# Queries and keys asked for two or three units ahead in a two-layer attention kernel

## The chip, the cores and the metric

The kernel runs on one core of a Trainium2 chip. The metric is device time in microseconds (us) of one execution of the whole program.

## What is computed

Two layers over 1024 latent tokens and 256 context tokens, model width 1024, all in fp32. Each layer is: adaptive norm, an input projection that also yields a gate, attention, gate, output projection, residual. Layer 0 is grouped-query attention (16 heads of 64 over 4 key heads, rotary positions, norms on queries and keys); there the context tokens attend too, to context only. Layer 1 is latent attention (16 heads, 64 + 32 wide). Cut to the attention, with the names of the reference:

```python
def gqa_attend(q, k, v):
    s = jnp.einsum('bqhgd,bkhd->bhgqk', q, k).astype(jnp.float32) * (GQA_HEAD_DIM ** -0.5)
    p = jax.nn.softmax(s, axis=-1).astype(v.dtype)
    return jnp.einsum('bhgqk,bkhd->bqhgd', p, v)

k_all = jnp.concatenate([kc, k], axis=1)
v_all = jnp.concatenate([vc, v], axis=1)
o = sweep_query_blocks(lambda qb: gqa_attend(qb, k_all, v_all), q).reshape(B, S, GQA_WIDTH)
y = (o * jax.nn.silu(g)) @ p["w_out"]
oc = gqa_attend(qc, kc, vc).reshape(B, L, GQA_WIDTH)
```

## The kernel before

Stages follow each other: modulation and norm, projections of layer 0 (queries, keys, values and gate go to DRAM), attention of layer 0, its output projection with the norm of layer 1, projections of layer 1, attention of layer 1, output projection. The change touches the two attention stages, which share the class `Attention`.

The work of attention is cut into **units**. Layer 0 has 20: 16 of one head with all 1024 latent queries against 10 key tiles of 128, and 4 short ones of context queries (one key head's four heads, 2 key tiles). The short ones stand at places 4, 9, 18 and 19, counted from 0; the first five units (0 to 4) share the first key head. Layer 1 has 16 units, each of one head and 10 key tiles.

Each unit needs two passes. First the **maxima**: for each of 8 blocks of 128 queries a product with the latent keys (`mx`, L364) whose rows VectorE reduces to a maximum (`mA`, L366), and two products with the context keys (L370, reduced to `mB`, L372); a context unit has only the last two. All use one PSUM tile. The maxima are transposed (L385), negated into a row (`crow`, L387) and written by DMA into an extra row of the unit's queries (L388), so that the second pass subtracts them inside the matmul. Second the **scores** (`st`, L423) key tile by key tile, the exponential on ScalarE (`p`, L426), sums over the keys on POOL (`acp`, L449) and VectorE (`acd`, L453), and the product with the values (`av`, L471). At a unit's end ScalarE copies `av` to `os` (L493, two buffers), TensorE spreads the sums over partitions (L515), ScalarE copies those to `rb` (L517), and by way of small DMAs (`cs` L519, `rrow` L524, `rb` L528), a reciprocal and two POOL products (L531, L532) the result is stored (`od`, L536).

TensorE's order is that of the program text; the other engines' orders are set by a scheduler. The loop `run` goes over pairs of key tiles; one key tile is a step. For each pair it asks `maxima` for all maxima up to `step - base + 1 + lead` (lead is 14), runs what has come due, issues the `av` of two pairs back, asks for one maximum more, and issues the scores of the pair. So the maxima run about a unit and a half ahead of the scores. `maxima` starts a unit, which means asking for its queries and keys, only when it has no maxima left in its list; and it starts none beyond the limit `t + 1 + ahead`, t being the place of the unit whose scores are issued and `ahead` 2. Since it starts a unit at the moment in which it needs it, its first `mx` follows the load directly in the program.

Queries are two tiles, QA (high halves twice, filled by two DMAs, L837) and QB (low halves and the row of maxima, L838) in layer 0; L846 and L847 are the same for context units. There are three sets of them (`qbufs=3`). Keys KA and KB are shared by the units of a key head (two sets). In layer 1 QH, QL, KH and KL belong to a unit (three sets, L1085 to L1091). All these DMAs are issued by SyncE's queue, in one order.

The transpose of the maxima writes into `spare`, the `av` tile of the unit that finished last, or into the `mx` tile when there is none yet. The spread sums of that same unit (L515) go into columns 0 to 255 of the same tile.

Of the kernel before, what the change touches and what calls it, by code (L numbers as in the profile page):

```python
# [14 lines left out]
ALU = mybir.AluOpType  # L15
# [4 lines left out]
P = 128  # L20
# [10 lines left out]
def raw(ap):  # L31
    return ap.bitcast(F32)
# [3 lines left out]
def hybrid_kernel(ctx: ExitStack, tc: tile.TileContext, ins: dict, out: bass.AP):  # L36
    nc = tc.nc
    pe, act, dve, pool, sp = nc.tensor, nc.scalar, nc.vector, nc.gpsimd, nc.sync
# [10 lines left out]
    ident = const.tile([P, P], F32, name="ident")  # L49
# [24 lines left out]
    def in_order(engine):  # L74

        return tc.manual_schedule(engines={engine})
# [240 lines left out]
    class Attention:  # L317
# [20 lines left out]
        def open_late(self, st, stp):  # L338
            l = self.l
            self.op = st.enter_context(tc.tile_pool(name=f"op{l}", bufs=2, reuse_waits="tile"))  # L340
            self.vp = stp.enter_context(tc.tile_pool(name=f"vp{l}", bufs=1 + l, reuse_waits="tile"))
            self.pp = stp.enter_context(tc.tile_pool(name=f"pp{l}", bufs=8, reuse_waits="tile"))
            self.ap = stp.enter_context(tc.tile_pool(name=f"ap{l}", bufs=2, reuse_waits="tile"))
            self.rd = st.enter_context(tc.tile_pool(name=f"rd{l}", bufs=4, space=DRAM))
            self.ps_s = stp.enter_context(tc.tile_pool(name=f"pss{l}", bufs=2, space=PSUM, reuse_waits="tile"))
            self.ps_o = stp.enter_context(tc.tile_pool(name=f"pso{l}", bufs=2, space=PSUM, reuse_waits="tile"))
# [27 lines left out]
        def do_shift(self, u):  # L374
            s = self.state[id(u)]
            c = s["mB"]
            if u["kind"] == "lat":
                c = self.sm.tile([P, 8], F32, name="mC", tag="mC")
                dve.tensor_max(c, s["mA"], s["mB"])

            def turn():
                t = self.spare
                if t is None:
                    t = self.ps_m.tile([P, 1024], F32, name="mx", tag="mx")
                pe.transpose(t[:8, :P], c, ident)  # L385
                r = self.sm.tile([8, P], F32R, name="crow", tag="crow")
                dve.tensor_scalar(r, t[:8, :P], -1.0, None, op0=ALU.mult)  # L387
                sp.dma_start(raw(s["crow"]), raw(r))  # L388

            self.later((2, turn))  # L390
# [13 lines left out]
        def maxima(self, upto, limit):  # L404

            while self.done < upto:
                if not self.todo:
                    if self.started >= min(limit, len(self.units)):
                        break
                    self.start_unit()  # L410
                u, m = self.todo.pop(0)
                self.done += 1
                self.do_max(u, m)
                if m == ("ctx", 1):
                    self.do_shift(u)
# [127 lines left out]
        def run(self, lead, ahead, extra):  # L543

            held = []
            base = self.step
            pairs = [(t, u, u["kts"][i:i + 2]) for t, u in enumerate(self.units) for i in range(0, len(u["kts"]), 2)]
            with in_order(mybir.EngineType.PE):
                for t, u, kts in pairs:
                    if kts[0] == u["kts"][0]:  # L550
                        for v in self.units[t:t + 2]:
                            self.load_v(v)
                    self.maxima(self.step - base + 1 + lead, t + 1 + ahead)
                    self.run_deferred(self.step)
                    if len(held) == 2:
                        self.do_av(*held.pop(0))
                    self.maxima(self.step - base + 2 + lead, t + 1 + ahead)
                    held.append((u, [(kt, self.do_scores(u, kt)) for kt in kts]))
                    if extra and self.step - base >= 5:
                        extra.pop(0)()  # L560
                    self.step += 2
                for h in held:
                    self.do_av(*h)
            self.run_deferred(self.step + self.lag)
# [250 lines left out]


    def l0_load(u, at):
        qp, kp = at.qp, at.kp
        g = u["g"]
        r = slice(64 * (g % 2), 64 * (g % 2) + 64)  # L820
        lat = u["kind"] == "lat"
        if g not in at.kcache:
            KA = kp.tile([P, NT], F32R, name="KA", tag="KA")
            KB = kp.tile([65, NT], F32R, name="KB", tag="KB")
            sp.dma_start(raw(KA[0:64, :]), k0h[g // 2, r, :])
            sp.dma_start(raw(KA[64:128, :]), k0l[g // 2, r, :])
            sp.dma_start(raw(KB[0:64, :]), k0h[g // 2, r, :])
            pool.memset(raw(KB[64:65, :]), 1.0)
            at.kcache[g] = dict(KA=KA, KB=KB)
        KA, KB = at.kcache[g]["KA"], at.kcache[g]["KB"]  # L830
        QA = qp.tile([P, NL], F32R, name="QA", tag="QA")
        QB = qp.tile([65, NL], F32R, name="QB", tag="QB")
        if lat:
            h = u["h"]
            r = slice(64 * (h % 2), 64 * (h % 2) + 64)
            for j in range(2):
                sp.dma_start(raw(QA[64 * j:64 * j + 64, :]), q0h[h // 2, r, :NL])  # L837
            sp.dma_start(raw(QB[0:64, :]), q0l[h // 2, r, :NL])  # L838
        else:
            for par in range(2):  # L840
                r = slice(64 * par, 64 * par + 64)
                cs = slice(512 * par, 512 * par + 512)
                sh = q0h[2 * g:2 * g + 2, r, NL:].rearrange("a p n -> p a n")
                sl = q0l[2 * g:2 * g + 2, r, NL:].rearrange("a p n -> p a n")
                for j in range(2):
                    sp.dma_start(raw(QA[64 * j:64 * j + 64, cs]).rearrange("p (a n) -> p a n", a=2), sh)  # L846
                sp.dma_start(raw(QB[0:64, cs]).rearrange("p (a n) -> p a n", a=2), sl)  # L847
        return dict(KA=KA, KB=KB, QA=QA, QB=QB, mq=QA, mk=KA, crow=QB[64:65, :])

    def l0_scores(s, kt):  # L850
        ks = slice(kt * P, (kt + 1) * P)
        return [(s["KA"][:, ks], lambda n: s["QA"][:, n * 512:(n + 1) * 512]),
                (s["KB"][:, ks], lambda n: s["QB"][:, n * 512:(n + 1) * 512])]
# [13 lines left out]
    def gate_path(l, c, w, hT, nt, ps_mm, wk):  # L867
        for m in range(4):
            for s0 in range(0, nt, 512):
                gate_slice(l, c, m, s0, min(512, nt - s0), w, hT, ps_mm, wk)  # L870

    at = Attention(0, units, dict(scale=0.125, load=l0_load, scores=l0_scores, kbufs=2, qbufs=3, vw=256))
    stE = ExitStack()
    with tc.tile_pool(name="wkg0a", bufs=4, **right) as wkg:
# [12 lines left out]
    pieces = []  # L887
    wo = [load_weight(ins["l0_w_out"], KT, 512 * n, 512, 0, todo=pieces) for n in range(2)]
    stL, stLP = ExitStack(), ExitStack()
    at.open_late(stL, stLP)  # L890
    at.run(14, 2, pieces)
    stLP.close()
    stE.close()

# [206 lines left out]
    for p_ in range(8):  # L1101
        for par in range(2):
# [3 lines left out]
    at = Attention(1, units, dict(scale=float(96 ** -0.5), load=l1_load, scores=l1_scores,  # L1106
                                  kbufs=3, qbufs=3, vw=128))
# [133 lines left out]
    pieces = []  # L1241
# [58 lines left out]
```

## Time and profile before

| what | value |
|---|---|
| median of 3 runs | 1938.57 us (1936.34 to 1942.59) |
| the profiled execution | 1934.7 us, span 1932.8 us |
| mean granted clock of TensorE | 0.971 |
| TensorE busy | 1806.6 us (93%) |
| attention of layer 0, 402 to 898 us | 495.41 us, TensorE busy 441.79 |
| attention of layer 1, 1357 to 1838 us | 481.00 us, TensorE busy 471.27 |

The page gives busy time by engine over one profiled execution. A window gives the same for a stretch. In a timeline each row is a group of instructions with its start, its duration and, in brackets, the idle time of the engine before it and what ended that. PE is TensorE, DVE VectorE, ACT ScalarE, POOL GpSimd, SP SyncE and SPq its queue of DMA issues. A releaser printed as "issue" means that the profile shows nothing that the engine waited for.

### The profile page before, as it was taken

To read this page: it belongs to the slowest core of one execution; us is meant where nothing else is said; L and a number is where in the kernel's file an instruction comes from. 1 tells how busy PE (TensorE), PEld (TensorE's weight loads), DVE (VectorE), ACT (ScalarE), POOL (GpSimd) and SP (SyncE) were. 2 spreads that over 40 slices of the span, in tenths; PEclk is the share of its full clock that TensorE was granted. 3 is DMA by queue.
4 is the path that set the end of the run, shared out by engine and by line. 5 is a ranking of instruction groups with operands and counts; after the bars stand their busy time and mean duration, and the time that the engine had idled before them with its cause. 6 is when DMAs were issued, how large, how long until landed. Compare 5 with 4: busy or idle time off the path is not lost. (4 is left out here: it accounts for less than half of the span.)

```text
span 1932.8 us, 23525 instructions
## 1 busy us (share of the span) xinstructions
PE 1806.6 (93%) x8360; PEld 1225.4 (63%) x8360; DVE 1003.9 (52%) x1494; ACT 633.1 (33%) x942; POOL 959.9 (50%) x648
## 2 busy tenths in 40 slices
PE   7889999988798899987998999999999999999999
PEld 3676668754344445543787889887555555555577
DVE  3754551355464566643456567765555454555332
ACT  2421221133233334432224453331433333333410
POOL 1553431156556467764224455342666657666521
PEclk9999999999898899998999999999999999999999
DMA  7556753332132222223443494766434334342152
GB/s 273 172 172 197 240 161 109 113 104 55 44 87 66 70 57 59 66 66 103 138 140 86 134 267 135 207 188 177 123 81 107 93 82 120 81 107 71 28 186 98
DMA packets 220765, 235.00 MB, mean 122 GB/s; under 512 B 34024, under 2 KB 162776, under 8 KB 220648
## 3 DMA queue, kind: packets, MB, share of 16 engines
q1 hardware_dynamic: 220648, 233.50, 42.7%
q8 instruction: 66, 1.08, 0.2%
q14 instruction: 51, 0.42, 0.1%
HBM read 159.51 MB, written 73.63 MB: 121 GB/s over the span
## 5 line engine op out<-in xcount | busy, mean ns | idle before, releaser
L366 DVE TENSOR_REDUCE mA<-mx 128x1 f32<-128x1024 f32 x256 | 313.3, 1224 | 378.2 <-PE mx L364 377.9
L426 ACT ACTIVATE p<-st 128x1024 f32<-128x1024 f32 x328 | 328.1, 1024 | 552.4 <-PE st L423 552.3
L449 POOL TENSOR_TENSOR acp<-acp,p 128x1024 f32<-128x1024 f32 x156 | 370.2, 2373 | 238.0 <-ACT p L426 232.5
L471 PE MATMUL av<-p,v 128*64 128x512 f32 x1312 | 330.7, 625 | 1.0 <-ACT rb L517 1.0
L129 POOL TENSOR_TENSOR wb<-wraw,wa 128x512 fp32r<-128x512 f32 (+3 forms) x69 | 90.6, 1332 | 175.8 <-ACT wa L148 175.2
L471 PEld LDWEIGHTS av<-p,v 128*64 128x64 f32 x1312 | 82.1, 140 | 149.6 <-issue 139.8
L364 PE MATMUL mx<-KA,QA 128*128 128x512 f32 x256 | 95.8, 458 | 40.2 <-DVE mA L366 14.5
L86 PE MATMUL mm<-wa,hh 128*128 128x512 f32 (+2 forms) x320 | 123.2, 385 | 2.5 <-ACT hh L286 2.5
L372 DVE TENSOR_REDUCE mB<-mx 128x4 f32<-128x1024 f32 x72 | 87.8, 1219 | 68.1 <-PE mx L370 67.8
L87 PE MATMUL mm<-wb,hh 128*128 128x512 f32 (+2 forms) x320 | 118.5, 371 | 0.0
L88 PE MATMUL mm<-wa,hl 128*128 128x512 f32 (+2 forms) x320 | 118.0, 370 | 0.0
L86 PE MATMUL y<-wa,oh 128*128 128x512 f32 x288 | 114.2, 396 | 3.5 <-ACT oh L594 3.5
L449 POOL TENSOR_TENSOR acp<-p 128x1024 f32<-128x1024 f32 x32 | 76.5, 2391 | 74.5 <-ACT p L426 73.8
L87 PE MATMUL y<-wb,oh 128*128 128x512 f32 x288 | 113.1, 393 | 0.0
L88 PE MATMUL y<-wa,ol 128*128 128x512 f32 x288 | 112.4, 391 | 0.0
L364 PEld LDWEIGHTS mx<-KA,QA 128*128 128x128 f32 x256 | 45.1, 203 | 103.2 <-DVE mA L366 52.4
L423 PE MATMUL st<-QA,KA 128*128 128x512 f32 x336 | 107.8, 402 | 0.0
L423 PE MATMUL st<-QB,KB 65*128 65x512 f32 x336 | 106.5, 398 | 0.0
L423 PE MATMUL st<-QH,KH 97*128 97x512 f32 x320 | 102.2, 400 | 1.3 <-DMA QH<-crow 1.3
L423 PE MATMUL st<-QL,KH 96*128 96x512 f32 x320 | 102.2, 400 | 0.6 <-DVE gth L311 0.6
L86 PE MATMUL mm<-hh,wa 128*128 128x512 f32 x256 | 102.2, 399 | 0.2 <-DVE qt L1182 0.2
L88 PE MATMUL mm<-hh,wb 128*128 128x512 f32 x256 | 101.8, 398 | 0.0
(212 smaller groups left out, 3383.9 us busy)
## 6 DMA issues: line engine op xcount, KB each, us to landing
mraw<-in_l_w_mod SPq DMA_DIRECT2D x96, 256.0 KB
wraw<-in_l_w_in SPq DMA_DIRECT2D x28, 512.0 KB
rb<-rrow SPq DMA_DIRECT2D x72, 128.0 KB
xt<-in_x SPq DMA_DIRECT2D x16, 512.0 KB
wraw<-in_l_w_out SPq DMA_DIRECT2D x16, 512.0 KB
sgd<-gth SPq DMA_DIRECT2D x32, 256.0 KB
QA<-q0h SPq DMA_DIRECT2D x32, 256.0 KB
sg<-sgd SPq DMA_DIRECT2D x64, 128.0 KB
```

The lines of the kernel that those rows point to most:

```text
L86: pe.matmul(ps, lhsT=lh(k), rhs=rh(k), start=first and i == 0, stop=False)
L87: pe.matmul(ps, lhsT=lh(k), rhs=rl(k), start=False, stop=False)
L88: pe.matmul(ps, lhsT=ll(k), rhs=rh(k), start=False, stop=last and i == len(ks) - 1)
L129: eng.tensor_sub(lo, a, b)
L364: pe.matmul(m[:, n * 512:(n + 1) * 512], lhsT=s["mq"][:, i * P:(i + 1) * P], rhs=s["mk"][:, n * 512:(n + 1) * 512], start=True, stop=True)
L366: dve.reduce_max(s["mA"][:, i:i + 1], m, axis=AX.X)
L372: dve.reduce_max(s["mB"][:, 4 * i:4 * i + 4], m.rearrange("p (a b) -> p a b", a=4), axis=AX.X)
L423: pe.matmul(ps[:, n * 512:(n + 1) * 512], lhsT=lh, rhs=rf(n), start=(j == 0), stop=(j == len(prods) - 1))
L426: act.activation(p, ps, AF.Exp, scale=self.ops["scale"])
L449: pool.tensor_add(t, a, p)
L471: pe.matmul(s["av"][64 * n:64 * n + 64, :], lhsT=s["v"][:, kt, u["vc"]:u["vc"] + 64], rhs=p[:, n * 512:(n + 1) * 512], start=kt == kts[0], ...
```

## The change

Four edits. In `run`, the first pair of each unit now starts all units up to the limit, before any maximum is asked for. In layer 0 `ahead` is 3 instead of 2, and a fourth set of queries is taken from a pool of its own: units 3, 7, 11 and so on use it. The transpose of the maxima goes to columns 256 to 383 of its tile. The loop in `maxima` is written differently and does the same.

```diff
         def open_late(self, st, stp):
             l = self.l
             self.op = st.enter_context(tc.tile_pool(name=f"op{l}", bufs=2, reuse_waits="tile"))
+            if not l:
+
+                self.qp2 = stp.enter_context(tc.tile_pool(name="qp0b", bufs=1, reuse_waits="tile"))
...
                 if t is None:
                     t = self.ps_m.tile([P, 1024], F32, name="mx", tag="mx")
-                pe.transpose(t[:8, :P], c, ident)
+                t = t[:8, 256:384]
+                pe.transpose(t, c, ident)
                 r = self.sm.tile([8, P], F32R, name="crow", tag="crow")
-                dve.tensor_scalar(r, t[:8, :P], -1.0, None, op0=ALU.mult)
+                dve.tensor_scalar(r, t, -1.0, None, op0=ALU.mult)
...
             while self.done < upto:
+                if not self.todo and self.started < min(limit, len(self.units)):
+                    self.start_unit()
                 if not self.todo:
-                    if self.started >= min(limit, len(self.units)):
-                        break
-                    self.start_unit()
+                    break
...
                         for v in self.units[t:t + 2]:
                             self.load_v(v)
+                        while self.started < min(t + 1 + ahead, len(self.units)):
+                            self.start_unit()
                     self.maxima(self.step - base + 1 + lead, t + 1 + ahead)
...
     def l0_load(u, at):
-        qp, kp = at.qp, at.kp
+        kp = at.kp
...
+        qp = at.qp if at.started % 4 < 3 else at.qp2
         QA = qp.tile([P, NL], F32R, name="QA", tag="QA")
...
     at.open_late(stL, stLP)
-    at.run(14, 2, pieces)
+    at.run(14, 3, pieces)
```

The last edit is layer 0's call; layer 1's stays at 2. The lines below L341 move down by 3 to 7 in the changed kernel (L364 is L367 there, L423 is L427, L837 is L844).

What the change does to TensorE's order, at the end of unit 2 in layer 0. Before, with `mB` the maxima of the context unit 4, and the six `mx` those of unit 5:

```order
L385 MATMUL av<-ident,mB 8x128
L471 MATMUL av<-p,v 64x512 x4
L423 MATMUL st<-QA,KA 128x512 x2
L423 MATMUL st<-QB,KB 128x512 x2
L423 MATMUL st<-QA,KA 128x512 x2
L423 MATMUL st<-QB,KB 128x512 x2
L364 MATMUL mx<-KA,QA 128x512 x6
L471 MATMUL av<-p,v 64x512 x4
L364 MATMUL mx<-KA,QA 128x512 x2
```

The same place after the change:

```order
L367 MATMUL mx<-KA,QA 128x512 x2
L389 MATMUL av<-ident,mB 8x128
L475 MATMUL av<-p,v 64x512 x4
L367 MATMUL mx<-KA,QA 128x512 x2
L427 MATMUL st<-QA,KA 128x512 x2
L427 MATMUL st<-QB,KB 128x512 x2
L427 MATMUL st<-QA,KA 128x512 x2
L427 MATMUL st<-QB,KB 128x512 x2
L367 MATMUL mx<-KA,QA 128x512 x2
L475 MATMUL av<-p,v 64x512 x4
```

The six matmuls of three maxima that stood together now stand two by two, the first four of them ahead of unit 2's last scores. It is the same at the ends of units 3, 7 and 8, and with the two context maxima of unit 19 at the end of unit 16.

SyncE's queue around the load of unit 5, with the numbers of the tiles. Before (cs and rrow and rb are those of unit 1; the two rows of maxima go to units 3 and 4; QA_3982 and QB_3983 are unit 5's):

```order
L519 DMA cs_3832<-rb_3827 32x1x8 x4
L388 DMA QB_3690<-crow_3919 1x8x128
L524 DMA rrow_3831<-cr_3948 128x8
L388 DMA QB_3895<-crow_3952 1x8x128
L528 DMA rb_3827<-rrow_3831 64x512 x2
L837 DMA QA_3982<-q0h_81 64x1024 x2
L838 DMA QB_3983<-q0l_82 64x1024
L536 DMA od0_96<-os_3825 64x512 x2
```

After (the first rows are those of unit 0; unit 5's queries are QA_3799 and QB_3800; the last cs is unit 1's):

```order
L523 DMA cs_3636<-rb_3631 32x1x8 x4
L392 DMA QB_3408<-crow_3722 1x8x128
L528 DMA rrow_3635<-cr_3759 128x8
L532 DMA rb_3631<-rrow_3635 64x512 x2
L844 DMA QA_3799<-q0h_81 64x1024 x2
L845 DMA QB_3800<-q0l_82 64x1024
L540 DMA od0_96<-os_3629 64x512 x2
L512 DMA sg_4048<-sgd0_94 64x512 x2
L523 DMA cs_3857<-rb_3852 32x1x8 x4
```

Unit 5's load has moved forward by one unit's DMAs: it stands behind unit 0's sums instead of unit 1's.

The transpose of unit 3's maxima and the spread sums ahead of it in TensorE's order, with the semaphores that each waits for. Before (av_3653 is unit 1's tile, av_3864 unit 2's; the mx is unit 4's):

```order
L515 MATMUL av_3653<-acp_3629,twos_76 32x256 [waits Pool_49]
L515 MATMUL av_3653<-acp_3629,twos_76 32x256 x3
L385 MATMUL av_3653<-ident_69,mC_3875 8x128 [waits DVE_49,Activation_49]
L471 MATMUL av_3864<-p_3842,v_3402 64x512 x2
L471 MATMUL av_3864<-p_3851,v_3402 64x512 x2
L370 MATMUL mx_3926<-KA_2934,QA_3894 128x256 [waits DMAHW4_49,DMAHW3_49,DVE_49]
```

After:

```order
L519 MATMUL av_3672<-acp_3648,twos_76 32x256 [waits Pool_49]
L519 MATMUL av_3672<-acp_3648,twos_76 32x256 x3
L389 MATMUL av_3672<-ident_69,mC_3900 8x128 [waits DVE_49,Activation_49]
L475 MATMUL av_3889<-p_3867,v_3405 64x512 x2
L475 MATMUL av_3889<-p_3876,v_3405 64x512 x2
L373 MATMUL mx_3942<-KA_2934,QA_3580 128x256 [waits DMAHW4_49,DMAHW3_49,DVE_49]
```

The order of these is unchanged, and the transpose names the same two semaphores, VectorE's and ScalarE's.

## Prediction

> **What bounds the kernel now.** I read the busy rows of the page first, then TensorE's waits, then the two attention stages as windows, and then the places of the waits in the timeline. The page gives busy time by engine, and the granted TensorE clock in 40 slices.
>
> ```profile
> PE 1806.6 (93%) x8360; PEld 1225.4 (63%) x8360; DVE 1003.9 (52%) x1494; ACT 633.1 (33%) x942; POOL 959.9 (50%) x648
> PEclk9999999999898899998999999999999999999999
> ```
>
> TensorE (PE) is the bound: 1806.6 of 1932.8 us. Eights stand among the nines in slices 11, 13, 14 and 19 (48.3 us each), so between 483 and 918 us PE runs slower at times. The two attention stages as windows (busy us of PE, PEld, DVE, ACT, POOL; then clock and DMA):
>
> ```profile
> 402.14:897.55 495.41, 441.79 (x1881) 233.39 (x1879) 273.79 (x276) 182.64 (x207) 317.30 (x154) 0.93 0.25 63
> 1357.00:1838.00 481.00, 471.27 (x2081) 278.06 (x2081) 244.92 (x262) 181.24 (x197) 314.42 (x158) 0.99 0.36 89
> 750.00:800.00 50.00, 48.70 (x218) 26.20 (x219) 31.79 (x34) 20.10 (x23) 36.06 (x19) 1.00 0.25 62
> ```
>
> Layer 1's attention leaves PE idle for 9.7 of 481 us. Layer 0's leaves it idle for 53.6 of 495.4 us, at clock 0.93; yet a stretch inside it (750 to 800) has 1.3 us of idle in 50 at clock 1.00. So layer 0 loses time in a few places. TensorE's waits name the candidates (total us, times, longest):
>
> ```profile
> PE mx L364 <- DVE mA L366: 14.9, 12, 1.3
> PE av L385 <- ACT rb L517: 13.4, 26, 0.9
> PE mx L364 <- DMA QA<-q0h: 8.9, 2, 4.5
> PE mx L364 <- issue: 8.8, 2, 4.5
> PE mx L370 <- DMA QA<-q0h: 4.5, 2, 3.1
> ```
>
> One such place in PE's timeline (start, duration; in brackets the idle before it), and the queue's Q load just ahead:
>
> ```profile
> 475.62 0.73 PE L423 MATMUL st<-QA,KA 128*128 128x512 f32 x2
> ...
> 482.24 1.19 PE L364 MATMUL mx<-KA,QA 128*128 128x512 f32 x2 [4.48 <-issue]
> 484.75 1.22 PE L364 MATMUL mx<-KA,QA 128*128 128x512 f32 x2 [1.32 <-DVE mA L366]
> 487.29 1.22 PE L364 MATMUL mx<-KA,QA 128*128 128x512 f32 x2 [1.32 <-DVE mA L366]
> 488.44 3.36 PE L471 MATMUL av<-p,v 128*64 128x512 f32 x8
> 491.73 0.73 PE L364 MATMUL mx<-KA,QA 128*128 128x512 f32 x2
> 492.30 0.62 PE L423 MATMUL st<-QA,KA 128*128 128x512 f32 x2
> ...
> 494.16 0.63 PE L364 MATMUL mx<-KA,QA 128*128 128x512 f32 x2
> 494.72 1.94 PE L471 MATMUL av<-p,v 128*64 128x512 f32 x8
> 496.59 0.72 PE L364 MATMUL mx<-KA,QA 128*128 128x512 f32 x2
> ```
>
> ```profile
> 452.12 1.29 SPq L846 DMA_DIRECT2D QA<-q0h  x2
> 477.32 1.08 SPq L837 DMA_DIRECT2D QA<-q0h  x2
> ```
>
> PE finishes a unit's last scores, then sits 4.48 us until the queries of unit 5, asked for at 477.32, have landed. Three maxima then follow with nothing between them, so that two wait 1.32 us each for VectorE's reduction, and the next eight av matmuls take 3.36 us where the same eight take 1.94 us later: after the stall PE is slow. The code says why three at once: the limit t+3 keeps unit 5 from starting during unit 2, the count falls behind, and the first call of unit 3 catches up. That is so only near the short context units (4 and 9), whose two maxima bring the next unit forward.
>
> **The change part by part.** First the price of one such place. The normal pair is 2 maxima, 1 av group, 1 score group. From the rows: a score group 494.16 - 492.30 = 1.86, a maximum 494.72 - 494.16 = 0.56, an av group 496.59 - 494.72 = 1.87. From 475.62 to 494.72 PE issued 2 score groups, 5 maxima and 1 av group: 3.72 + 2.80 + 1.87 = 8.4 us of work at full speed. This stretch and the three others cut at the same instructions, and a fifth at the end of the stage:
>
> ```profile
> 475.62:494.72 19.10, 11.99 (x37) 5.90 (x35) 4.89 (x4) 3.19 (x4) 12.59 (x7) 0.73 0.34 83
> 511.76:531.35 19.59, 12.49 (x36) 6.04 (x34) 4.89 (x4) 3.18 (x4) 12.94 (x8) 0.74 0.33 80
> 610.80:630.24 19.44, 12.48 (x36) 6.10 (x34) 4.90 (x4) 3.18 (x4) 12.58 (x7) 0.74 0.32 81
> 647.29:665.86 18.57, 11.49 (x36) 5.88 (x34) 4.89 (x4) 3.18 (x4) 12.93 (x8) 0.72 0.34 85
> 850.76:865.07 14.31, 9.79 (x34) 5.38 (x33) 2.45 (x2) 2.62 (x3) 12.58 (x7) 0.76 0.29 80
> ```
>
> Four stretches: 19.10 + 19.59 + 19.44 + 18.57 = 76.70, less 4 x 8.4 = 33.6, leaves **43.1 us** (7.1 us of plain idle each, the rest slow matmuls). The fifth holds 2 score groups, 1 av group and the two maxima of a context unit:
>
> ```profile
> 856.00 0.71 PE L370 MATMUL mx<-KA,QA 128*128 128x256 f32 x4 [3.10 <-DMA QA<-q0h]
> 858.12 1.19 PE L370 MATMUL mx<-KA,QA 128*128 128x256 f32 x4 [1.42 <-DMA QA<-q0h]
> ```
>
> At 0.58 us per such maximum (estimate: 4 x 256 columns, as many as the 2 x 512 that took 0.56) it is 3.72 + 1.87 + 1.16 = 6.8 us of work, and 14.31 - 6.8 = **7.5 us** lost.
>
> *The limit of layer 0 raised by one, the loop that starts units at a unit's beginning, and the fourth query set* go together. PE's order after the change has one maximum either side of each av group at all five places, so bursts are gone. In the queue, unit 5's Q load takes the slot that unit 4's had: issued at 452.12 before, some 21 us ahead of its first maximum, which would come at about 473.6. A 4.9 us load (477.32 to 482.24) is hidden by that. The fourth set is what makes it possible: the load now waits for the scores of unit 1, not of unit 2. I take the whole 43.1 + 7.5 = 50.6 us. Nothing else is late at once in place of the load: in 750 to 800 the same pattern runs with POOL busy 36.06 of 50, DVE 31.79, and PE idle 1.3. At the fifth place POOL could hold the gain back, since it lags behind at the end of layer 0:
>
> ```profile
> 849.17 9.65 POOL L449 TENSOR_TENSOR acp<-acp,p 128x1024 f32<-128x1024 f32 x4 [4.17 <-ACT p L426]
> 869.54 2.36 POOL L449 TENSOR_TENSOR acp<-p 128x1024 f32<-128x1024 f32 x1 [5.97 <-ACT p L426]
> ```
>
> But it then sat idle 5.97 us waiting for p. Moved up by 7.5 us that sum would start at 862.0, and POOL is free at 869.54 - 5.97 = 863.6: 1.6 us late for one sum, made up before the next. So the fifth counts in full.
>
> *The same loop in layer 1* has three sets of keys and queries and the old limit. There the loads wait for their buffers anyway:
>
> ```profile
> 1416.26 0.31 SPq L1091 DMA_DIRECT2D QL<-q1l  x1
> 1418.70 1.13 SPq L536 DMA_DIRECT2D od<-os  x2
> 1419.88 0.59 SPq L1085 DMA_DIRECT2D KH<-k1h  x1
> ```
>
> ```profile
> PE av L385 <- ACT rb L517: 7.5, 14, 0.9
> ```
>
> The order moves KH, QH and KL ahead of one od store: some 3 us earlier, a full unit before they are used, and the store some 3 us later at most. The second fence is the only wait of PE listed between 1400 and 1800 us; none names a load. I take 0.
>
> *The transposed maxima in columns 256 to 383.* Before, the transpose (L385) waits for ScalarE's copy of the sums (13.4 us in 26 waits), for both use columns 0 to 127 of one tile. After, the columns are apart, but the order with its waits still shows the ScalarE semaphore on every one of them. I take 0; if the wait went, it would be 13.4 us less. [...]
>
> *The rewritten loop in maxima* tests the same things in another order and issues nothing.
>
> *What the moved loads pass.* Each is 3 DMAs (6 for a context unit), no more than before. At units 2, 3, 7 and 8 they now stand between the two halves of rb or ahead of an od store, while SyncE waits for PE's scores (total, times, longest):
>
> ```profile
> SPq L837 <- PE st L423: 33.0, 11, 6.9
> 524.85 1.13 SPq L536 DMA_DIRECT2D od<-os  x2
> 538.24 0.59 ACT L493 COPY os<-av 128x512 f32<-128x512 f32 x1 [1.32 <-PE av L471]
> ```
>
> The copy at 538.24 (unit 4's) needs the store issued at 524.85 (unit 2's), 13.4 us earlier. With the stall of 511.76 to 531.35 gone the copy comes 11.2 us sooner and the store does not: 2.2 us are left for the landing, and ScalarE's exps queue behind that copy. In the new order the copy stands one exp later (over 1 us). I take 0; the bounds are 0 and the longest such wait, 6.9 us, at units 4 and 9: 13.8 us.
>
> **Sum.** The profiled execution took 1934.7 us (span 1932.8): 1934.7 - 50.6 = 1884.1. The median of the runs shown, 1938.57, is 3.9 above it; the measured median should be about **1888.0 us**. A change of 0.3% (6 us) is what a measurement of this kernel tells from none.
>
> **Rivals.** (a) *Part is given back.* The late store above costs up to 13.8 us. Also, two waits of 2.4 us stand where VectorE is late behind POOL's sums after a context unit, and each slows the next group:
>
> ```profile
> 574.76 0.73 PE L364 MATMUL mx<-KA,QA 128*128 128x512 f32 x2 [2.39 <-DVE mB L372]
> 576.77 3.57 PE L471 MATMUL av<-p,v 128*64 128x512 f32 x8
> ```
>
> That is 2.39 + (3.57 - 1.94) = 4.0 us each. Four more of them would cost 16 us; either or both give 1896 to 1918, say 1904. For it: POOL catches up in the present stalls (12.6 us busy in each). Against: 750 to 800 keeps step without any. Chance 0.16. (b) *The transposes stop waiting*: 1888.0 - 13.4 = 1874.6. Against it stand the waits in the order. 0.05. (c) *The change does not do what it says*: the early load still waits for a buffer until the burst, and all stays: 1938.6. Against it, the load stands one unit's work earlier in the order. 0.03. (d) *Slower*: every Q load of layer 0 that waits for a buffer, 16 of them (units 4 to 19), holds SyncE's queue; the rb and od DMAs behind it come late, POOL's sums queue behind the rb product, and p buffers run out. At 6.9 us each that is 16 x 6.9 = 110 us, 1888 + 110 = 1998; it decides from 50.6 / 16 = 3.2 us per load. The mean wait now is 33.0 / 11 = 3.0 us, but PE lost none of it in 750 to 800. 0.04.
>
> **The numbers.** The forecast, 1880 to 1896, has 0.72. The range 1874 to 1908 holds it, (b), and some half of (a): about 0.85. Faster by over 0.3%: 0.72 + 0.16 + 0.05 = 0.93; within 0.3%: 0.03; slower: 0.04.
>
> **What would show it.** Right: in layer 0's running stage no maximum with a bracket naming DMA QA or a 4.4 us issue; no run of three maxima; the stage's window some 50 us shorter at clock 0.98 or more; the 2.4 us waits on mB still two. The wait of the transposes on ScalarE stays at about 0.5 us, 26 times; if it is gone, (b). If a wait on an av group, on st behind os, or on mB appears new after units 4 and 9, (a). What would make me wrong is a wait in layer 0 that today's stalls cover and that I did not find; layer 1 and all stages outside attention should stay within 2 us.

## The result, and the profile after

The changed kernel takes 1890.99 us (median of 4 runs, 1887.21 to 1898.05), the kernel before 1938.59 (4 runs, 1936.34 to 1942.59). The ratio is 0.9756, with a 95% interval of 0.9723 to 0.979. The forecast was 1888.0 in a range of 1874 to 1908.

In the changed kernel's file the lines stand three or four further down: L364 is L367, L366 L369, L372 L375, L385 L389, L423 L427, L449 L453, L453 L457, L471 L475, L517 L521. The page's rows that answer to those of before:

```profile
PE 1788.6 (95%) x8360; PEld 1218.9 (65%) x8360; DVE 1008.3 (53%) x1494; ACT 632.8 (34%) x942; POOL 964.5 (51%) x648
PEclk8999999999999999998999999998999999999999
```

The eights of slices 11, 13 and 14 are gone; those that stand now, in slices 1, 19 (849 to 897 us) and 28, lie outside layer 0's attention but for the last 3 us of it. The stages as windows (span, then busy us of PE, PEld, DVE, ACT, POOL, the clock, DMA), cut where the stages of the changed kernel begin:

```profile
402.00:852.00 450.00, 425.20 (x1880) 229.32 (x1878) 279.59 (x276) 182.00 (x207) 320.07 (x153) 0.98 0.28 71
852.00:1311.50 459.50, 433.01 (x2229) 370.24 (x2229) 271.48 (x559) 157.78 (x331) 179.14 (x206) 0.97 0.57 164
1311.50:1792.00 480.50, 470.81 (x2081) 278.23 (x2081) 242.90 (x263) 181.96 (x198) 315.39 (x157) 0.99 0.35 89
```

Layer 0's attention takes 450.0 us, 45.4 less than the 495.41 of before, at a granted clock of 0.98 in place of 0.93; layer 1's 480.5 (before 481.0); the stage between the two was 1357.00 - 897.55 = 459.45 and is 459.5. The whole span went from 1932.8 to 1887.5, 45.3. So the gain lies in one stage. Where TensorE ran three maxima in a row after a 4.48 us wait, it now runs one maximum on either side of each av group:

```profile
475.61 0.62 PE L427 MATMUL st<-QA,KA 128*128 128x512 f32 x2
...
477.48 0.63 PE L367 MATMUL mx<-KA,QA 128*128 128x512 f32 x2
477.94 0.27 PE L389 MATMUL av<-ident,mB 128*8 128x128 f32 x1
478.14 1.94 PE L475 MATMUL av<-p,v 128*64 128x512 f32 x8
480.01 0.73 PE L367 MATMUL mx<-KA,QA 128*128 128x512 f32 x2
480.58 0.62 PE L427 MATMUL st<-QA,KA 128*128 128x512 f32 x2
```

and the queries of unit 5 were asked for at 456.05, 21.4 us ahead of that first maximum at 477.48:

```profile
456.05 1.08 SPq L844 DMA_DIRECT2D QA<-q0h  x2
```

TensorE's waits after: no row names QA or "issue" for a maximum any more; the transposes' wait stays.

```profile
PE av L389 <- ACT rb L521: 13.2, 26, 0.9
PE mx L367 <- DVE mB L375: 5.8, 3, 2.3
PE mx L367 <- DVE mA L369: 4.8, 6, 1.3
PE mx L389 <- DVE mA L369: 2.7, 1, 2.7
```

The last row is new: before, no transpose waited longer than 1.3 us for mA. It belongs to the first 35 us of layer 0's attention, the one stretch of the table below that is over 0.6 us longer in the changed kernel. The same transpose before, and TensorE there after:

```profile
417.05 0.27 PE L385 MATMUL mx<-ident,mC 128*8 128x128 f32 x1 [1.32 <-DVE mA L366]
417.25 1.94 PE L471 MATMUL av<-p,v 128*64 128x512 f32 x8
```

```profile
415.87 0.73 PE L367 MATMUL mx<-KA,QA 128*128 128x512 f32 x2 [1.11 <-DVE mB L375]
419.32 0.37 PE L389 MATMUL mx<-ident,mC 128*8 128x128 f32 x1 [2.73 <-DVE mA L369]
419.63 3.48 PE L475 MATMUL av<-p,v 128*64 128x512 f32 x8
```

**One row for each unit.** ScalarE copies the spread sums of every unit once (`rb`, 36 copies in each profile), so the starts of these copies give a clock by units. From them, and from TensorE's third score group of the stage (412.95 before, 412.72 after), come four spans for each kernel, in us: from that score group to the first copy (start), from the first copy to the 18th (layer 0), from there to the 21st (between), and to the 36th (layer 1). (Two expectations call that score group the fourth; it is the same row.)

| kernel | start | layer 0 | between | layer 1 |
|---|---|---|---|---|
| before | 29.67 | 454.77 | 507.96 | 435.44 |
| changed | 33.83 | 405.44 | 508.52 | 435.29 |
| before_again | 29.70 | 454.71 | 507.96 | 435.44 |
| loop_only | 34.31 | 455.37 | 510.96 | 435.28 |
| columns_only | 29.56 | 453.45 | 511.03 | 435.47 |
| no_loop | 34.73 | 409.92 | 507.16 | 435.30 |
| bursts_kept | 33.46 | 422.12 | 507.25 | 435.28 |
| no_columns | 33.81 | 406.90 | 511.50 | 434.72 |
| first_late | 33.46 | 403.91 | 509.34 | 435.26 |
| mc_one_input | 32.07 | 410.25 | 506.65 | 435.26 |
| turn_later | 30.98 | 405.62 | 516.21 | 425.82 |
| both | 31.70 | 404.04 | 515.88 | 425.83 |
| turn_l1 | 33.58 | 405.35 | 510.57 | 425.82 |
| held_load | 34.22 | 406.65 | 514.85 | 425.82 |

The change gains 454.77 - 405.44 = 49.3 us in layer 0 and loses 4.2 at its start: 2.5 of these as longer idle time of TensorE (3.84 us in that stretch, 1.32 before), the rest as slow matmuls such as the 3.48 us above. The experiments ask which edit carries the 49.3, how it splits, and what makes the 4.2.

### The profile page after: what moved, and what is told of

Its sections match the earlier page's. It is cut to its first block, busy times and chain, and to the rows that moved or that the text cites. A ratio compares the mean times of both kernels' runs of the same rounds, so it can differ in the third digit from the quotient of the medians.

```text
span 1887.5 us, 23536 instructions
## 1 busy us (share of the span) xinstructions
PE 1788.6 (95%) x8360; PEld 1218.9 (65%) x8360; DVE 1008.3 (53%) x1494; ACT 632.8 (34%) x942; POOL 964.5 (51%) x648
## 5 line engine op out<-in xcount | busy, mean ns | idle before, releaser
L369 DVE TENSOR_REDUCE mA<-mx 128x1 f32<-128x1024 f32 x256 | 313.4, 1224 | 340.5 <-PE mx L367 340.5
L453 POOL TENSOR_TENSOR acp<-acp,p 128x1024 f32<-128x1024 f32 x156 | 371.4, 2381 | 235.6 <-ACT p L430 230.0
L475 PE MATMUL av<-p,v 128*64 128x512 f32 x1312 | 324.9, 615 | 1.7 <-ACT rb L521 1.7
L475 PEld LDWEIGHTS av<-p,v 128*64 128x64 f32 x1312 | 80.9, 138 | 146.8 <-issue 136.6
L375 DVE TENSOR_REDUCE mB<-mx 128x4 f32<-128x1024 f32 x72 | 87.8, 1220 | 63.1 <-PE mx L373 63.1
L427 PE MATMUL st<-QA,KA 128*128 128x512 f32 x336 | 106.8, 399 | 0.0
L427 PE MATMUL st<-QB,KB 65*128 65x512 f32 x336 | 106.3, 398 | 0.0
L427 PE MATMUL st<-QH,KH 97*128 97x512 f32 x320 | 102.2, 400 | 1.0 <-DMA QH<-crow 1.0
L427 PE MATMUL st<-QL,KH 96*128 96x512 f32 x320 | 102.4, 401 | 0.6 <-DVE gth L311 0.6
L87 PE MATMUL mm<-hl,wa 128*128 128x512 f32 x256 | 101.9, 398 | 0.0
L367 PE MATMUL mx<-KA,QA 128*128 128x512 f32 x256 | 89.0, 429 | 13.3 <-DVE mB L375 5.8
L427 PE MATMUL st<-QH,KL 96*128 96x512 f32 x320 | 99.7, 393 | 0.0
```

The source lines that it names most:

```text
L87: pe.matmul(ps, lhsT=lh(k), rhs=rl(k), start=False, stop=False)
L367: pe.matmul(m[:, n * 512:(n + 1) * 512], lhsT=s["mq"][:, i * P:(i + 1) * P], rhs=s["mk"][:, n * 512:(n + 1) * 512], start=True, stop=True)
L369: dve.reduce_max(s["mA"][:, i:i + 1], m, axis=AX.X)
L375: dve.reduce_max(s["mB"][:, 4 * i:4 * i + 4], m.rearrange("p (a b) -> p a b", a=4), axis=AX.X)
L427: pe.matmul(ps[:, n * 512:(n + 1) * 512], lhsT=lh, rhs=rf(n), start=(j == 0), stop=(j == len(prods) - 1))
L453: pool.tensor_add(t, a, p)
```

## The experiments

Each was timed against the kernel before on the same chip; ratios are to that kernel.

**The loop alone** on the kernel before.

```diff
                             self.load_v(v)
+                        while self.started < min(t + 1 + ahead, len(self.units)):
+                            self.start_unit()
```

> The kernel before with the early start loop alone (two units ahead, three query sets, limit t+3 unchanged in effect). Theory (the early load needs the fourth query set to be early, and the limit still holds the maxima back): the 4.5 us waits for QA after units 2, 3, 7 and 8 and the pairs of 1.32 us stay, layer 0's attention stays near 495 us, 1935 to 1942 us. Rival (asking early is what counts, the set matters little): the QA waits go, 1888 to 1905 us.

Measured: 1938.17 us (10 runs, 1935.06 to 1941.54), ratio 0.9986 (0.9973 to 0.9999). The waits of before are all there:

```profile
PE mx L364 <- DVE mA L366: 14.9, 12, 1.3
PE mx L364 <- issue: 8.8, 2, 4.4
PE mx L364 <- DMA QA<-q0h: 8.7, 2, 4.4
```

Asking early brings next to nothing (0.14%) while the limit is t+3 and a third set is the last. The rival falls.

**The fourth set and the limit, without the loop.**

```diff
-                        while self.started < min(t + 1 + ahead, len(self.units)):
-                            self.start_unit()
```

> The changed kernel without the early start loop: fourth query set and the limit t+4 alone. Theory (the set and the limit carry the gain; the maxima() order starts the next unit soon enough): the loop is not needed in the middle of layer 0, and as unit 3's queries are no longer asked for ahead of the stage's first pairs, the 4.1 us lost at its start come back: 1884 to 1890 us. Rival (without the loop each load is asked for only when its first maximum is due): QA waits of up to 4.5 us come back at every unit of layer 0 and some of layer 1, over 1910 us.

Measured: 1896.75 us (5 runs, 1889.22 to 1897.01), ratio 0.976 (0.9739 to 0.9781); the profiled execution 1889.98. No wait for QA came back, so the set and the limit together carry the gain and the loop is not what brings it; no run has one of the two alone. The trace of layer 0 is 4.5 us longer than with the loop (409.92 against 405.44), 2.4 of it in one unit; the times cannot tell that, and their median lies above the 1884 to 1890 of the theory. The start did not get better (34.73), and unit 3's queries were still asked for before the stage (398.51 us), though the text no longer asks for them there: the order of the queue is the scheduler's. That half of the theory fell.

**The bursts kept.** The loads are as early as in the changed kernel, but the maxima are held by the old limit.

```diff
+                if limit < len(self.units) and any(self.todo[0][0] is x for x in self.units[limit:]):
+                    break
                 u, m = self.todo.pop(0)
...
-                    self.maxima(self.step - base + 1 + lead, t + 1 + ahead)
+                    self.maxima(self.step - base + 1 + lead, t + 3)
```

(the second call of `maxima` alike)

> The changed kernel, with the maxima held by the old limit t+3: the queries lie there early, but three maxima still follow each other after units 2, 3, 7 and 8. Splits the price of 10.8 us a place (4.5 us wait for the queries; two waits of 1.32 us for VectorE; the rest slow matmuls). Theory (the wait for the queries is the larger part and it brings the slow matmuls): the QA waits are gone, two waits of 1.32 us remain at four places, 4 x 2.6 = 10.6 us and a slow group at some: 1898 to 1912 us. Rival (the burst alone slows TensorE as before): 1920 to 1934 us.

Measured: 1908.41 us (5 runs, 1904.09 to 1913.27), ratio 0.9841 (0.9821 to 0.9862). One of its four places:

```profile
480.87 0.63 PE L367 MATMUL mx<-KA,QA 128*128 128x512 f32 x2
482.82 0.73 PE L367 MATMUL mx<-KA,QA 128*128 128x512 f32 x2 [1.32 <-DVE mA L369]
484.87 1.22 PE L367 MATMUL mx<-KA,QA 128*128 128x512 f32 x2 [1.32 <-DVE mA L369]
486.02 3.68 PE L477 MATMUL av<-p,v 128*64 128x512 f32 x8
```

Two stretches of this trace as windows, ahead of the burst and over that av group:

```profile
474.00:480.80 6.80, 6.80 (x33) 4.06 (x30) 2.08 (x5) 2.56 (x3) 3.41 (x2) 1.00 0.15 35
486.02:489.70 3.68, 3.68 (x10) 0.84 (x9) 1.23 (x1) 0.00 (x0) 3.68 (x3) 0.50 0.02 4
```

The wait for the queries is gone, the two of 1.32 us are there, and the next av group is slow (3.68 us against 1.94, at a granted clock of 0.50 where it was 1.00 ahead of the burst) though no wait was longer than 1.32. Of the 49.3 us of layer 0, the early queries bring 454.77 - 422.12 = 32.7 and the spreading of the maxima 422.12 - 405.44 = 16.7. The theory holds: two thirds are the wait and what follows it, one third is the burst.

**The columns**, alone on the kernel before, and taken out of the changed kernel. The question is whether the 26 waits of the transposes on ScalarE's copy, 13.4 us before, go when transposes and sums no longer share columns.

```diff
-                pe.transpose(t[:8, :P], c, ident)
+                t = t[:8, 256:384]
+                pe.transpose(t, c, ident)
...
-                dve.tensor_scalar(r, t[:8, :P], -1.0, None, op0=ALU.mult)
+                dve.tensor_scalar(r, t, -1.0, None, op0=ALU.mult)
```

> The kernel before with the transposed maxima in columns 256 to 383, nothing else. [...] Rival (columns of their own free the transposes): the 26 waits go, 1922 to 1928 us.

> The changed kernel with the transposed maxima back in columns 0 to 127. Theory (the columns do nothing): same as the changed kernel, 1888 to 1894 us, 26 waits of 0.5 us on ScalarE as there. Rival (columns of their own save something that the waits do not show): 1895 us or more.

Measured: columns_only 1941.36 us (12 runs, 1935.12 to 1946.24), ratio 1.0001 (0.9986 to 1.0016), and the wait is the same:

```profile
PE av L386 <- ACT rb L518: 13.4, 26, 0.9
```

no_columns 1894.10 us (4 runs, 1891.69 to 1895.08), ratio 0.9761 (0.9743 to 0.9779), beside 0.9756 for the changed kernel. The columns bring nothing that can be measured, in either kernel.

**Unit 3 not started at the stage's first unit.**

```diff
-                        while self.started < min(t + 1 + ahead, len(self.units)):
+                        while t and self.started < min(t + 1 + ahead, len(self.units)):
```

> The changed kernel, but the early start loop is left out at the stage's first unit, so unit 3's keys and queries are not asked for ahead of the weights there. Theory (that load, put ahead of the last w_out piece, and the weight casts that slide with it, cost the 4.1 us at the stage's start): the 2.73 us wait for the reduction mA and the slow av group after it at 419 go, 1885 to 1889 us. Rival (the start is late for another reason): the 4.1 us stay, 1890 to 1893 us.

Measured: 1891.38 us (5 runs, 1889.65 to 1896.14), ratio 0.9757 (0.9738 to 0.9777). The experiment missed: `maxima` starts unit 3 in the loop's place, and on every engine the instructions stand as in the changed kernel (the wait for mA is 2.74 us), so it decides nothing on the start. It is the changed kernel once more, and tells how well its time repeats, 1890.99 and 1891.38, and a trace: layer 0 took 403.91 us here and 405.44 there.

**The transposes one pair later**, alone and with the edit above (which changes no order, so that the two are one kernel run twice). The question is whether the 26 waits, 13.2 us in the changed kernel, go when other work stands between the spread and the transpose; all of it gained would be 1890.99 - 13.2 = 1877.8 us.

```diff
-            self.later((2, turn))
+            self.later((4, turn))
```

> The changed kernel with each transpose of the maxima run one pair later, so that it does not stand right behind the spreading of the sums. [...] Rival (the row of maxima then reaches the queries too late, and PE waits for its scores): 1891 to 1930 us.

> The two edits before it together: no early start at the stage's first unit, transposes one pair later. [...]

Measured: turn_later 1891.03 us (4 runs, 1889.13 to 1893.71), ratio 0.9748 (0.973 to 0.9766); both 1888.65 (4 runs, 1883.95 to 1892.42), ratio 0.9734 (0.9712 to 0.9755). The 26 waits on ScalarE's copy are gone from the list and layer 1 is 9.5 us shorter (425.82 against 435.29), about 0.65 us for each steady unit. It is given back: the first unit of layer 1 waits 5.03 us for its row of maxima,

```profile
1331.85 1.19 PE L427 MATMUL st<-QH,KH 97*128 97x512 f32 x2 [5.03 <-DMA QH<-crow]
```

and in layer 0 units 3 and 8 each lose 3.8 us (29.64 against 25.79 from copy to copy in unit 3). There VectorE's two sums took 4.43 us instead of 1.28 with GpSimd's operations beside them, and TensorE waited for the reduction queued behind them:

```profile
519.18 2.38 POOL L453 TENSOR_TENSOR acp<-acp,acd 128x1024 f32<-128x1024 f32 x1
519.36 4.43 DVE L457 TENSOR_TENSOR acd<-p 128x512 f32<-128x512 f32 x2
...
521.51 1.73 POOL L536 TENSOR_TENSOR os<-os,rb 128x512 f32<-128x512 f32 x1
...
524.98 1.20 PE L367 MATMUL mx<-KA,QA 128*128 128x512 f32 x2 [2.41 <-DVE mA L369]
```

**VectorE beside GpSimd.** The same pattern stands at the start of the changed kernel's stage. The row of `mC` before, and the rows of VectorE and GpSimd (POOL) after:

```profile
414.98 0.17 DVE L379 TENSOR_TENSOR mC<-mA,mB 128x8 f32<-128x8 f32 x1
```

```profile
411.52 3.15 DVE L457 TENSOR_TENSOR acd<-p 128x512 f32<-128x512 f32 x2
...
412.39 3.40 POOL L129 TENSOR_TENSOR wb<-wraw,wa 128x512 fp32r<-128x512 f32 x2
...
415.76 2.35 POOL L453 TENSOR_TENSOR acp<-acp,p 128x1024 f32<-128x1024 f32 x1
415.84 2.29 DVE L382 TENSOR_TENSOR mC<-mA,mB 128x8 f32<-128x8 f32 x1
...
419.19 1.28 DVE L457 TENSOR_TENSOR acd<-acd,p 128x512 f32<-128x512 f32 x2
```

`mC`, of 8 columns, starts 0.08 us after GpSimd's sum and ends with it, 2.29 us later; in the first profile of before it took 0.17. Behind it in VectorE's order stands the reduction `mA` that empties the `mx` tile, into which the transpose writes: so TensorE's wait names mA. Of the 32 `mC` in the changed kernel's trace, the 4 that ran beside a GpSimd operation took 1.06 to 2.29 us and the other 28 at most 0.17. The next kernel tests whether its two inputs are what makes mC late there: mA and mB lie in one tile, and mC is a reduction with that one input.

```diff
-                dve.tensor_max(c, s["mA"], s["mB"])
+                dve.reduce_max(c, s["mAB"].rearrange("p (a b) -> p b a", a=2), axis=AX.X)
...
-                s["mA"] = self.sm.tile([P, 8], F32, name="mA", tag="mA")
-            s["mB"] = self.sm.tile([P, 8], F32, name="mB", tag="mB")
+                s["mAB"] = self.sm.tile([P, 16], F32, name="mAB", tag="mAB")
+                s["mA"], s["mB"] = s["mAB"][:, :8], s["mAB"][:, 8:]
+            else:
+                s["mB"] = self.sm.tile([P, 8], F32, name="mB", tag="mB")
```

> The changed kernel with the maximum mC made by a reduction over one tile that holds mA and mB side by side, in place of an operation with two tiles as inputs. Theory (VectorE's operations with two SBUF inputs stand still while GpSimd's run, its reductions do not): mC at the stage's start falls from 2.29 us to about 0.2 us though a GpSimd sum runs beside it, the transpose's wait for mA there falls from 2.73 to about 1.3 us, and all 32 mC from 10.6 us to about 6; 2 to 4 us off the start, 1886 to 1890 us. Rival (mC is late for its inputs or its queue): it stays over 1.5 us there, 1891 us.

```profile
418.54 2.35 POOL L455 TENSOR_TENSOR acp<-acp,p 128x1024 f32<-128x1024 f32 x1 [1.19 <-ACT p L432]
419.07 0.17 DVE L382 TENSOR_REDUCE mC<-mAB 128x8 f32<-128x16 f32 x1
...
421.14 0.37 PE L389 MATMUL mx<-ident,mC 128*8 128x128 f32 x1 [1.32 <-DVE mAB L369]
```

With the same sum beside it mC takes 0.17 us, and the transpose waits 1.32 us, not 2.73; all 32 take 5.45 us in sum, not 10.61, and none over 0.17. So beside GpSimd's sum the form with two inputs was held up (2.29 us) and the one with a single input was not (0.17). The start falls by 1.8 us only (32.07), 1.7 of it idle time of TensorE, and `acd` still meets GpSimd (3.24 us there). The time does not fall: 1890.72 us (5 runs, 1886.17 to 1894.03), ratio 0.9736 (0.9718 to 0.9753). Layer 0 took 410.25 us, 4.8 more than in the changed kernel, for elsewhere sums met worse; after the context unit at place 4:

```profile
553.80 6.68 DVE L459 TENSOR_TENSOR acd<-p 128x512 f32<-128x512 f32 x2
...
561.68 1.22 PE L367 MATMUL mx<-KA,QA 128*128 128x512 f32 x2 [4.65 <-DVE mAB L375]
```

where the changed kernel had 4.36 and 2.33. The unit behind it took 3.3 us longer, and the one behind the context unit at place 9 2.6.

**Is the start's loss the change's?** The kernel before, profiled again, without any edit:

> The kernel before, once more with a profile. Theory (the start of layer 0's attention is lost or not by how VectorE's and GpSimd's operations happen to meet, not by the change): the time from the fourth score group to the first spread of the sums, 29.67 us in the first profile of it, can come out at 33 to 35 us here too, as in the kernel with the loop alone. Rival (the change's early load makes it): 29.7 us again, within 0.5.

It took 1938.35 us (one run), and 29.70 us for the start. The rival's number came. But loop_only, which has no early load and whose queue issues the same loads there as before, has 34.31. So the last kernel holds unit 3's load back.

```diff
                 dve.tensor_max(c, s["mA"], s["mB"])
+                [act.copy(self.qp2.tile([n, NL], F32R, name=q, tag=q)[:, :8], c[:n, :]) for q, n in (("QA", P), ("QB", 65)) if not self.l and u is self.units[1]]
...
-                    self.maxima(self.step - base + 1 + lead, t + 1 + ahead)
+                    self.maxima(self.step - base + 1 + lead, t + 1 + ahead - (not self.l and not t))
```

(the loop and the second call alike; the base is turn_l1, below)

> The kernel with the transposes later in layer 1, and unit 3's queries of layer 0 held back: two small ScalarE copies (128x8 and 65x8, overwritten by the load) keep the fourth set's buffer taken until unit 1's maxima are made, and the limit is one lower for the stage's first unit. In the order the two weight casts then stand after two exps as before the change, and all weight differences of GpSimd ahead of its first sum. Theory (the early load pushes the weights back, so that GpSimd's differences meet VectorE's sums and mC): the time from the fourth score group to the first spread falls from 33.6 to about 29.7 us, mC there is 0.2 us and not 2.29, and 4 us less in all, 1878 to 1882 us. Rival (the order of the weights is not what decides): 33 us or more, 1883 us or more.

Measured: 1887.20 us (5 runs, 1882.41 to 1887.86), ratio 0.9729 (0.971 to 0.9749). The load came at 416.86, the weights' differences stand ahead of GpSimd's first sum as before the change, and the start still takes 34.22 us, with 1.47 us for mC:

```profile
407.96 2.52 POOL L129 TENSOR_TENSOR wb<-wraw,wa 128x512 fp32r<-128x512 f32 x2 [1.49 <-ACT wa L148]
...
410.44 2.38 POOL L453 TENSOR_TENSOR acp<-p 128x1024 f32<-128x1024 f32 x1
410.74 3.24 DVE L457 TENSOR_TENSOR acd<-p 128x512 f32<-128x512 f32 x2
```

In the kernel before:

```profile
407.00 2.52 POOL L129 TENSOR_TENSOR wb<-wraw,wa 128x512 fp32r<-128x512 f32 x2 [1.06 <-ACT wa L148]
410.29 2.36 POOL L449 TENSOR_TENSOR acp<-p 128x1024 f32<-128x1024 f32 x1 [0.77 <-ACT p L426]
411.75 2.06 DVE L453 TENSOR_TENSOR acd<-p 128x512 f32<-128x512 f32 x2
```

There the VectorE sum started 1.46 us behind GpSimd's, in held_load 0.30, and it took 2.06 us there and 3.24 in held_load. My theory fell: the early load is not needed for the loss. What the kernels with the loss share is that VectorE's operations with two inputs meet GpSimd's for longer: mC took 1.47 us in held_load, 1.66 in loop_only and 2.29 in the changed kernel and in no_loop, and 0.17 in both profiles of before and in columns_only. Two ways lead there: the weights' differences behind the first sum (changed kernel), or ahead of it but late against TensorE, since the last weight piece had not landed (ScalarE waited 1.31 us for it in loop_only and 1.50 in held_load, 0.50 in before_again). In both profiles of before, as in columns_only, which has no loss, TensorE ran score rows ahead of this place in 1.05 us where held_load's took 0.63; that this slowness spared them the meeting fits the times, but no run isolates it.

The pace is the granted clock: 0.50 over such rows of before (403.45 to 404.73), before_again, columns_only and no_columns, 1.00 over those of held_load (402.67 to 404.54), loop_only and no_loop. The table can be read by it. Without the early load the start is 29.56 to 29.70 where those score rows took 1.05 us (the two profiles of before, columns_only) and 34.22 to 34.31 where they took 0.63 (held_load, loop_only). With it the weights' differences stand behind the first sum in all nine profiles, and where neither mC nor layer 0's transposes were edited the start is 33.46 to 34.73 at either pace (no_columns 1.05 us and 33.81, no_loop 0.63 us and 34.73). So beside the slow pace the change costs some 4 us, beside the fast one about none. Why the clock is low at the stage's start in some profiles and not in others, and how the runs without a profile went, stays open, and with it how much of the 4.2 us belongs to the change. (In the profiles held_load is 4.3 us longer than turn_l1 between the stages, 514.85 against 510.57; its higher median goes that way.)

**Layer 1's transposes alone one pair later**, its first unit left as it was:

```diff
-            self.later((2, turn))
+            self.later((4 if self.l and u is not self.units[0] else 2, turn))
```

> The changed kernel with the transposes one pair later in layer 1 alone, its first unit left as it was. Theory (in the run with all transposes later each steady unit of layer 1 took 0.65 us less, which was given back at the first unit of layer 1, 5.0 us for the row of maxima, and at units 3 and 8 of layer 0, 3.85 us each): 14 units x 0.65 = 9 us less and nothing given back, 1880 to 1884 us. Rival (the give-back comes from the later row in any unit, or moves to the end of the stage): 1888 to 1893 us.

Measured: 1883.79 us (4 runs, 1882.26 to 1890.28), ratio 0.9711 (0.9691 to 0.9731). Layer 1 keeps its 9.5 us (425.82), 2.1 are given back between the stages (510.57 against 508.52), and the profiled execution is 1882.3 against 1889.58. The transpose behind another av group waits for nothing:

```profile
1421.25 0.64 PE L519 MATMUL av<-acp,twos 128*32 128x256 f32 x8
1421.82 1.94 PE L475 MATMUL av<-p,v 128*64 128x512 f32 x8
1427.51 0.27 PE L389 MATMUL av<-ident,mC 128*8 128x128 f32 x1
```

The theory holds for layer 1, but for what is given back between the stages, and this version is faster than the kernel before and, by its trace and its median, than the changed one. Its interval meets the 0.9723 to 0.979 of the changed kernel's own runs at the edge, and lies below that of first_late (0.9738 to 0.9777), the same instructions with 5 runs.

## Why the prediction was right, and where not

- **The price of four places, 43.1 us.** Right: from the transpose at 443.04 before (446.97 after) to the one at 844.17 (806.15), the stage went from 401.13 to 359.18 us, 41.95 less. The missing 1.1 are four new waits for mA, 0.22 to 0.34 us each, 1.1 in sum. bursts_kept bears out the makeup: with the queries there early, the 8 waits of 1.3 us (10.5 in sum) and slow groups behind them are most of what is left.
- **The fifth place, 7.5 us, "counts in full".** Right: 53.38 us became 46.00, 7.4 less. GpSimd's lag did not hold it back.
- **Three edits together.** Set and limit together carry the gain (no_loop), and the loop without them brings next to nothing (loop_only). That the load needs the fourth set, as the prediction says, was not tested by itself. What the loop itself brings is 4.5 us in no_loop's trace, which the times cannot confirm; the prediction did not part the three.
- **Transposes 0, the loop of layer 1 0, maxima 0.** Right: 26 waits, 13.2 us; layer 1 435.29 against 435.44. That the wait would stay was read from the order, where its semaphore still stood; columns_only shows the same 13.4 us on the kernel before, so it is not the shared columns, which the prediction names, that the wait hangs on. Since the semaphore stayed, no run shows whether the hardware needs that wait.
- **What the moved loads pass, 0.** The feared late store did not come: TensorE's wait of the spread for ScalarE's `os` copy is 12.0 us in 3 after, 13.2 in 3 before, and those copies waited for a store twice in each, 20.2 us after and 21.1 before. The two 2.4 us waits for mB stayed two.
- **The step that failed** is the start of the stage. The prediction's sum has no term for it: it looked for what the loads pass on SyncE's queue and what waits behind them, and took the sums of VectorE beside GpSimd's as work that keeps step, as between 750 and 800 us. Its rival (a) had VectorE late behind GpSimd's sums, but only after context units. The changed kernel lost 4.2 us at the start, with the two engines' operations there on each other: mC took 2.29 us for 0.17. That the meeting makes such waits is shown by mc_one_input (1.32 us where the changed kernel waits 2.73); that the change makes the meeting is shown only against the slow pace of before. With the 1.1 above, 1884.1 + 4.2 + 1.1 = 1889.4; the profiled execution took 1889.58.
- **The median.** The forecast carried the 3.9 us between the profiled execution and the median of before over to the changed kernel; there it was 1890.99 - 1889.58 = 1.4. By luck that cancelled 2.5 of the 5.5 us by which the profiled execution missed 1884.1.

## What to carry to other kernels

Price a stall by the whole stretch against the same instructions at full speed, since here 3.7 of 10.8 us were slow matmuls behind the waits; and when a load comes late, look whether its consumers also bunch, for a third of layer 0's gain was the bunch. Before counting a stretch as undisturbed, look where VectorE's operations with two SBUF inputs fall on GpSimd's: their durations, not their busy shares, show it (2.29 us instead of 0.17 for mC, up to 6.68 instead of 1.28 for a pair of sums). A wait that stands in the program's order as a semaphore can be covered by other work in between, as in turn_l1, where layer 1 became 9.5 us shorter; what that work delays showed itself here at the first unit of the next stage (5.03 us) and at units 3 and 8 of layer 0 (3.8 us each, turn_later).

## What the runs showed of the hardware

- An 8-column maximum of two SBUF tiles on VectorE took 0.17 us alone and 2.29 with a GpSimd sum beside it, and a pair of 128x512 sums 1.28 alone and up to 6.68 beside GpSimd's operations; a reduction with one input beside the same sum took 0.17 (after, mc_one_input).
- TensorE's next av group was slow (3.68 us instead of 1.94, granted clock 0.50) after two waits of 1.32 us with 0.73 us of matmul between them, 2.64 us of idle time in sum (bursts_kept). Ahead of these waits the clock was 1.00.
